# Weight slots and modulated halves moved onto the address grid of the feed-forward tiles

## The chip, the cores and the metric

One NeuronCore of one Trainium2 chip runs the whole program. The metric is device microseconds of one execution, the median of several; the executions of the kernel before lie between 2122.51 and 2123.18 us. The profile is one further execution with the hardware profiler on.

## What is computed

Four decoder layers over 256 tokens of width 1024, in float32. Each layer has three sub-layers: a SwiGLU feed-forward, a token mixer (latent attention, differential attention, Mamba-2, latent attention in layers 0 to 3), and a second feed-forward. Every sub-layer modulates its input by columns that come from a condition vector, and ends in a LayerNorm:

```
def _swiglu(h, w_in, w_out):
    gate, up = jnp.split(h @ w_in, 2, axis=-1)
    return (jax.nn.silu(gate) * up) @ w_out

def _sublayer(x, fn, mod_j, g, b, weight):
    shift, scale, gate = mod_j[:, 0, None, :], mod_j[:, 1, None, :], mod_j[:, 2, None, :]
    y = fn(x * (1 + scale) + shift)
    return _layernorm(DEEPNORM_ALPHA * x + weight * gate * y, g, b)
```

The feed-forward is 1024 to 2 x 2816 and 2816 to 1024, eight times in all. These products, and the mixers' projections, are nearly all of the work.

## The kernel before

**Layout of the data.** Activations lie transposed: features on the 128 partitions, the 256 tokens along the free axis, eight blocks k of 128 features. A matrix product in near-float32 precision is made of three fp32r matmuls (`mm3`, line 475): each operand is split into a high half and a low half, and high x high, high x low and low x high are summed in PSUM. In the rows of the profile the moving operand stands first behind the arrow and the weights second: `mm<-hwh,wr` moves a modulated high half over a weight block.

**The tiles that matter.** `wraw` receives raw weights from HBM. `wr` has 16 slots of 4,096 bytes a partition, each with the high or the low half of four k of one 256-column piece of weights; a matmul takes a block of 128 columns, 512 bytes, so every block starts a multiple of 512 bytes into its slot. `hwh` and `hwl` hold the high and low half of a sub-layer's modulated input, eight rows k one behind the other. `g` has 25 slots of 2,048 bytes, and each half of a feed-forward's hidden tile (two k of 1,024 bytes) fills one; mixers keep their tiles there too.

**Joint first products.** The statistics of a LayerNorm are known late. So the first product of a sub-layer runs on the unnormalized sum, with 258 columns: 256 tokens and two boundary columns that carry the scale and shift terms (`pre_mms`, line 860). `Tail.chunk` writes these wide rows, the boundary columns among them from `abcol` (two strided 128x8 writes for each half). Later, `normalize` (line 847) overwrites the same tiles with the finished modulated input of 256 columns, and all other first products of the sub-layer read that. Before the change both kinds of row start every HP = 288 elements, 1,152 bytes. The very first sub-layer has no joint product; `first_group` (line 698) writes 256-column rows and issues, for each k, 36 matmuls (two halves of the weights, three pieces, two column blocks, three products).

**Order.** All operations are recorded, and a planner with a table of costs lays them out on the engines; the program is then issued in that order. Semaphore waits are set by the framework from what the instructions read and write. First products of a later feed-forward run k by k: in each k six matmuls for one weight piece (two column blocks of three), 12 where two pieces run together. Output products sum over the 22 hidden blocks of 128, three matmuls for each.

**Addresses.** The pools are laid one behind the other in the order in which the code makes them, and the first, `g`, starts at a byte that is 128 modulo 1,024. The slots of `g`, `wraw`, `gacc`, `res`, `t256`, `sd` and `re` are multiples of 1,024 bytes, so all of these start at that remainder. Then come `dtr` (512 bytes), `w0` (128), two `mrows` of 512 and six `modc` of 96: 2,240 bytes, which is 2 x 1,024 + 192. So `wr`, `hwh` and `hwl` start 192 bytes further, at 320 modulo 1,024, and row k of a modulated half starts 128k bytes further again (1,152 = 1,024 + 128).

Of the kernel before, what the change touches and what calls it, by code (L numbers as in the profile page):

```python
# [11 lines left out]
F32R = mybir.dt.float32r  # L12
# [8 lines left out]
S = 256  # L21
L = 4
KD = D // 128
# [396 lines left out]
def trunk(ctx: ExitStack, tc: tile.TileContext, consts, x, c, positions, w_mod, b_mod, ln_g, ln_b,  # L420
# [10 lines left out]
    PW, HP = S + 2, 288  # L431
    slots = {}

    def pool(name, n, elems, dt=F32):
        slots[name] = Slots(sb, name, n, elems, dt=dt, fresh=name == "g")

    slots["mm"] = slots["aux"] = Slots(pp, "mm", 8, 512, True)
    for name, n, elems in (("g", 25, 512), ("wraw", 8, 1024), ("gacc", 1, 1024), ("res", 1, 2048),
                           ("t256", 14, 256), ("sd", 1, 512), ("re", 1, 512), ("dtr", 1, 128), ("w0", 1, 32),
                           ("mrows", 2, 128), ("modc", 6, 24)):  # L440
        pool(name, n, elems)
    for name, n, elems in (("wr", 16, 1024), ("hwh", 1, KD * HP), ("hwl", 1, KD * HP)):
        pool(name, n, elems, F32R)

    def buf(tag, shape, dt=F32):
        return slots[tag].tile(shape, dt)
# [10 lines left out]
    def mmbank(name="pmm"):  # L457
        return buf("mm", [128, 2, 256])

    def aux(name="paux"):  # L460
        return buf("aux", [128, 512])

    def g2(dt=F32, name="g2"):
        return buf("g", [128, 2, 256], dt)
# [4 lines left out]
    def t256(dt=F32, name="t256"):  # L469
        return buf("t256", [128, 256], dt)  # L470

    def f(ap):
        return ap.bitcast(F32)
# [20 lines left out]
    def copy(out, in_):  # L494
        prog.alt((A, "activation", (), dict(out=out, in_=in_, func=AF.Copy)), (V, "tensor_copy", (), dict(out=out, in_=in_)))

    def split(src, hi, lo):
        A.activation(out=hi, in_=src, func=AF.Copy)
        (V.tensor_tensor if src.root.slots.psum else tt)(out=lo, in0=src, in1=f(hi), op=ALU.subtract)

    P_ = {}
    items = []
# [136 lines left out]
    modc = {}  # L639
# [58 lines left out]
    def first_group(res):  # L698

        modc[0] = buf("modc", [128, 24])  # L700
        gm_state["mac"] = 16
        hh, hl = buf("hwh", [128, KD, HP], F32R)[:, :, :S], buf("hwl", [128, KD, HP], F32R)[:, :, :S]
        banks = [mmbank("pf") for _ in range(2 * G0)]
        xr = None
        wv = ffn_w_in[0, 0].rearrange("(k p) (a c) -> k p a c", p=128, a=2)
        for k in range(KD):
            if k % 2 == 0:
                xr = g2(name="xin")
                prog.slack = 0.0 if k else SOON
                Q.dma_start(out=xr, in_=x[0, :, k * 128:k * 128 + 256].rearrange("(t p) c -> p t c", p=128))  # L710
                prog.slack = 0.0
            t = []
            for h in range(2):
                t.append(buf("wraw", [128, 4, 2, 128]))
                for a in range(2):
                    c0 = a * 1024 + k * 128
                    Q.dma_start(out=t[h][:, :, a], in_=w_mod[0, h * 512:h * 512 + 512, c0:c0 + 128].rearrange("(j p) c -> p j c", p=128))
            pg = aux("pgm0")
            prog.bundle(1100.0, [dict(out=pg[32 * (j % 4):32 * (j % 4) + 32, :256], lhsT=condc[:, j:j + 1].to_broadcast([128, 32]),
                                      rhs=t[j // 4][:, j % 4].rearrange("p a c -> p (a c)"), start=(j < 4), stop=(j >= 4)) for j in range(8)])  # L720
            row = t256(name="row0")
            copy(row, pg[:, :256])
            pc = aux("pc0")
            for a in range(2):
                TL.matmul(out=pc[:, a:a + 1], lhsT=row[:, a * 128:a * 128 + 128], rhs=inv32, start=True, stop=True)
            sc = sm_cols[:, k]
            V.scalar_tensor_tensor(out=sc[:, 0:1], in0=pc[:, 1:2], scalar=1.0, in1=bmodc[:, 8 + k:9 + k], op0=ALU.add, op1=ALU.add)
            V.tensor_tensor(out=sc[:, 1:2], in0=pc[:, 0:1], in1=bmodc[:, k:k + 1], op=ALU.add)
            px = aux("pxT")
            for tk in range(2):  # L730
                TL.transpose(px[:, tk * 128:tk * 128 + 128], xr[:, tk, (k % 2) * 128:(k % 2) * 128 + 128], ident)
            A.activation(out=res[:, k], in_=px[:, :S], func=AF.Copy, scale=ALPHA)
            h = t256(name="h")
            V.tensor_scalar(out=h, in0=px[:, :S], scalar1=sc[:, 0:1], scalar2=sc[:, 1:2], op0=ALU.mult, op1=ALU.add)
            split(h, hh[:, k], hl[:, k])
            for a in range(2):
                raw = buf("wraw", [128, G0 * 256])
                Q.dma_start(out=raw, in_=wv[k, :, a, :G0 * 256])
                wh, wl = buf("wr", [128, G0 * 256], F32R), buf("wr", [128, G0 * 256], F32R)
                split(raw, wh, wl)  # L740
                for b in range(G0):
                    for c in range(2):
                        c0 = b * 256 + c * 128
                        mm3(banks[2 * b + a][:, c], wh[:, c0:c0 + 128], wl[:, c0:c0 + 128], hh[:, k], hl[:, k],
                            k == 0 and c == 0, k == KD - 1 and c == 1)
        return hh, hl, banks

    class Tail:
# [4 lines left out]
        def chunk(self, m, ps):  # L753
# [23 lines left out]
            if self.s + 1 == NS:  # L777
                if m == 0:
                    self.banks = [[buf("mm", [128, 512]) for _ in range(2)] for _ in range(2)]
                    self.grow, self.brow = buf("wraw", [128, D]), buf("gacc", [128, D])  # L780
                    Q.dma_start(out=self.grow, in_=ln_g[L - 1, 2:3, :].to_broadcast([128, D]))
                    Q.dma_start(out=self.brow, in_=ln_b[L - 1, 2:3, :].to_broadcast([128, D]))
                dg = t256(name="dg")
                A.activation(out=dg, in_=d[:, m], func=AF.Copy, scale=P_["lngc"][:, self.s * 8 + m:self.s * 8 + m + 1])
                for t in range(2):
                    TL.transpose(self.banks[t][m // 4][:, (m % 4) * 128:(m % 4) * 128 + 128], dg[:, t * 128:t * 128 + 128], ident)
            else:
                first = DEFER.get(self.s, 0)
                if m < first:
                    return  # L790
                if m == first:
                    self.ab = boundary_cols(self.s + 1)
                    self.w = [buf("hw" + n, [128, KD, HP], F32R)[:, :, :PW] for n in "hl"]
                    for q in range(2):
                        A.activation(out=self.w[0][:, :, S + q], in_=self.ab[:, q], func=AF.Copy)
                        V.tensor_tensor(out=self.w[1][:, :, S + q], in0=self.ab[:, q], in1=f(self.w[0][:, :, S + q]), op=ALU.subtract)
                for j in range(0 if m == first else m, m + 1):
                    a = self.ab[:, 0, j:j + 1]
                    A.activation(out=self.w[0][:, j, :S], in_=d[:, j], func=AF.Copy, scale=a)
                    V.scalar_tensor_tensor(out=self.w[1][:, j, :S], in0=d[:, j], scalar=a, in1=f(self.w[0][:, j, :S]),  # L800
                                           op0=ALU.mult, op1=ALU.subtract)
# [37 lines left out]
    class Enter:  # L839
        def __init__(self, s, tail, res):  # L840
            self.s, self.res, self.tail = s, res, tail
            self.ab = tail.ab
            self.wh, self.wl = tail.w
            tail.stats()
            self.R, self.E = tail.re[:, 0], tail.re[:, 1]

        def normalize(self, need_h=True):
            u, ab = self.res, self.ab
            if need_h:
                self.hh, self.hl = self.wh[:, :, :S], self.wl[:, :, :S]  # L850
            for m in range(KD):
                tt(out=u[:, m], in0=u[:, m], in1=self.R, op=ALU.mult)
                tt(out=u[:, m], in0=u[:, m], in1=self.E, op=ALU.add)
                if need_h:
                    h = t256(name="h")
                    act_affine(h, u[:, m], ab[:, 0, m:m + 1], ab[:, 1, m:m + 1])
                    split(h, self.hh[:, m, :S], self.hl[:, m, :S])
            for m in range(KD):
                act_affine(u[:, m], u[:, m], ab[:, 2, m:m + 1], ab[:, 3, m:m + 1])
        def pre_mms(self, *ws):  # L860
# [730 lines left out]
    tail, res = None, buf("res", [128, KD, S])  # L1591
    for s in range(NS):
        en = Enter(s, tail, res) if s else None
        kind = "ffn" if s % 3 != 1 else MIXERS[s // 3]
        tail = Tail(s, res, 0.5 if kind == "ffn" else 1.0)
# [35 lines left out]
```

## Time and profile before

| | us |
|---|---|
| median of three runs | 2123.11 |
| the profiled execution, its own time | 2126.3 |
| its span, first to last instruction | 2124.5 |
| TensorE matmuls busy | 2097.0 (99%) |
| VectorE busy | 1723.4 (81%) |
| ScalarE busy | 1186.8 (56%) |
| moved from and to HBM | 504.73 MB, 238 GB/s in the mean |

Matmuls overlap in the engine, and the end of each is modelled. So the length that the profile lists for one is longer than the time until the next one starts, and the busy share says little of how fast TensorE goes. What tells it is the distance from one start to the next, which is read from the timeline: a row there gives the start of a run of equal instructions, its length and their number. All instructions stand on line 396, the one line that issues them; groups are told apart by tile names.

### The profile page before, as it was taken

What the parts mean: (1) busy time and instruction counts of PE and PEld (TensorE: products, weight loads), DVE (VectorE), ACT (ScalarE), POOL (GpSimd) and SP (SyncE); (2) the same over time, 40 slices, a digit from 0 to 9 for tenths busy, and PEclk for the clock granted to TensorE, in tenths of its full rate; (3) what the DMA queues carried; (4) which work ended last, traced back from release to release, by engine and by line L of the source; (5) the groups of instructions that cost most, each with busy time, mean ns of one, the idle gap of its engine ahead of it and who ended that gap; (6) DMA issues with size and microseconds to landing.
All of it is one profiled execution on the core that took longest, in us unless ns stands there. A gap on an engine that the chain in (4) does not pass through costs nothing.

```text
span 2124.5 us, 43163 instructions
## 1 busy us (share of the span) xinstructions
PE 2097.0 (99%) x17398; PEld 2027.6 (95%) x17398; DVE 1723.4 (81%) x2739; ACT 1186.8 (56%) x1853; POOL 96.0 (5%) x112
## 2 busy tenths in 40 slices
PE   8999999999999999999999999999999999999998
PEld 6999999999999999999999988899999999999998
DVE  3788999878887868978987898879887888879744
ACT  3553687446544776544644575547545644577543
POOL 0000110000000101000000011000000000100000
PEclk9999999999999999999999999999999999999999
DMA  9899667887899534899588744345897789545851
GB/s 293 275 330 327 216 209 247 291 305 217 280 315 319 174 103 148 302 314 314 191 304 308 249 141 143 115 156 196 303 315 226 258 309 316 178 131 187 258 184 55
DMA packets 410636, 504.73 MB, mean 238 GB/s; under 512 B 22073, under 2 KB 371652, under 8 KB 410436
## 3 DMA queue, kind: packets, MB, share of 16 engines
q1 hardware_dynamic: 410436, 501.98, 71.4%
q8 instruction: 136, 2.23, 0.4%
q14 instruction: 64, 0.52, 0.1%
HBM read 500.73 MB, written 1.05 MB: 236 GB/s over the span
## 4 chain that ended last, share of the span: by engine, by line
PE 93%; DVE 4%; issue 1%; ACT 1%; DMA 0%; POOL 0%; SPq 0%; DVEq 0%; POOLq 0%; ACTq 0%
PE mm L396 93%; DVE res L396 1%; DVE t L396 1%; DVE wr L396 1%; DVE sd L396 0%; DVE g L396 0%; DVE hwl L396 0%; DMA wraw<-in_w_mod_dram 0%; ACT t L396 0%; ACT g L396 0%; ACT wr L396 0%; SPq L396 0%; POOL rs L396 0%; ACT L396 0%; DVE gacc L396 0%
## 5 line engine op out<-in xcount | busy, mean ns | idle before, releaser
L396 PE MATMUL mm<-hwh,wr 128*128 128x256 f32 (+1 forms) x6736 | 1234.7, 284 | 3.7 <-ACT hwh L396 1.9
L396 PEld LDWEIGHTS mm<-hwh,wr 128*128 128x128 f32 x6736 | 1045.4, 189 | 24.4 <-issue 18.2
L396 ACT ACTIVATE wr<-wraw 128x1024 fp32r<-128x1024 f32 (+3 forms) x705 | 700.7, 1003 | 621.1 <-DMA wraw<-in_ffn_w_in_dram 190.4
L396 PE MATMUL mm<-hwl,wr 128*128 128x256 f32 (+1 forms) x3368 | 960.1, 285 | 3.3 <-DVE hwl L396 3.1
L396 DVE TENSOR_TENSOR wr<-wraw,wr 128x1024 fp32r<-128x1024 f32 (+3 forms) x693 | 796.8, 1167 | 166.7 <-ACT wr L396 160.3
L396 PE MATMUL mm<-g,wr 128*128 128x256 f32 x5496 | 671.6, 281 | 1.6 <-DVE g L396 0.9
L396 PEld LDWEIGHTS mm<-g,wr 128*128 128x128 f32 x5496 | 655.0, 188 | 11.8 <-issue 6.9
L396 PEld LDWEIGHTS mm<-hwl,wr 128*128 128x128 f32 x3368 | 637.6, 189 | 9.2 <-DVE hwl L396 5.1
L396 DVE SCALAR_TENSOR_TENSOR gacc<-wraw,condc,gacc 128x1024 f32<-128x1024 f32 x238 | 305.9, 1285 | 4.7 <-DMA wraw<-in_w_mod_dram 2.2
L396 ACT ACTIVATE g<-mm 128x512 f32<-128x512 f32 (+4 forms) x209 | 105.4, 517 | 51.0 <-PE mm L396 49.2
L396 ACT ACTIVATE g<-g 128x512 fp32r<-128x512 f32 (+1 forms) x104 | 63.7, 625 | 37.8 <-DVE g L396 37.3
L396 PE MATMUL mm<-g,g 128*128 128x128 f32 (+2 forms) x464 | 81.8, 312 | 0.0
L396 DVE TENSOR_TENSOR g<-g,g 128x512 fp32r<-128x512 f32 (+2 forms) x114 | 75.3, 686 | 3.4 <-ACT g L396 2.3
L396 DVE TENSOR_TENSOR res<-res,re 128x256 f32<-128x256 f32 x168 | 66.9, 420 | 8.6 <-ACT re L396 8.2
L396 POOL TENSOR_TENSOR res<-res,t 128x256 f32<-128x256 f32 x31 | 28.4, 943 | 914.9 <-ACT t L396 914.9
L396 DVE TENSOR_TENSOR g<-g,mm 128x512 f32<-128x512 f32 x81 | 54.4, 682 | 14.9 <-PE mm L396 14.5
L396 ACT ACTIVATE t<-mm 128x256 f32<-128x256 f32 (+1 forms) x72 | 27.1, 377 | 68.8 <-PE mm L396 68.5
L396 PEld LDWEIGHTS mm<-g,g 128*128 128x128 f32 (+1 forms) x464 | 57.9, 175 | 7.2 <-ACT g L396 0.4
L396 ACT ACTIVATE t<-res 128x256 f32<-128x256 f32 x84 | 34.6, 416 | 51.9 <-DVE res L396 42.2
L396 DVE SCALAR_TENSOR_TENSOR res<-mm,gw,res 128x256 f32<-128x256 f32 x84 | 39.5, 478 | 16.9 <-PE mm L396 16.4
L396 ACT ACTIVATE t<-res,abcol 128x256 f32<-128x256 f32 x72 | 43.1, 599 | 8.1 <-DVE res L396 6.8
L396 ACT ACTIVATE res<-res,abcol 128x256 f32<-128x256 f32 x88 | 47.5, 589 | 0.0
(200 smaller groups left out, 1165.1 us busy)
## 6 DMA issues: line engine op xcount, KB each, us to landing
wraw<-in_ffn_w_in_dram SPq DMA_DIRECT2D x340, 512.0 KB
wraw<-in_w_mod_dram SPq DMA_DIRECT2D x272, 512.0 KB
wraw<-in_ffn_w_out_dram SPq DMA_DIRECT2D x128, 512.0 KB
wraw<-in_ffn_w_out_dram SPq DMA_DIRECT2D x64, 384.0 KB
wraw<-in_ssm_w_in_dram SPq DMA_DIRECT2D x32, 512.0 KB
wraw<-in_diff_w_in_dram SPq DMA_DIRECT2D x24, 512.0 KB
wraw<-in_w_mod_dram SPq DMA_DIRECT2D x32, 256.0 KB
wraw<-in_mla_w_out_dram SPq DMA_DIRECT2D x16, 512.0 KB
```

Of the source, the lines that this page charges most:

```text
L396: getattr(eng.real, method)(*[real(a) for a in args], **{k: real(v) for k, v in one.items()})
```

## The change

The four pools whose sizes are no multiple of 1,024 bytes (`dtr`, `w0`, `mrows`, `modc`) are made after `wr`, `hwh` and `hwl` instead of before. These three start 192 bytes lower, at 128 modulo 1,024 as `g` does. A new function `modulated()` makes each of the two modulated tiles once and gives two views of it: wide rows of 258 columns every 1,152 bytes, for the joint products, and narrow rows of 256 columns every 1,024 bytes, for everything else. `normalize`, `first_group` and all first products after the joint ones use the narrow rows; the joint products use the wide rows as before. Wide and narrow rows share the same bytes.

```diff
@@ -436,11 +436,12 @@
     for name, n, elems in (("g", 25, 512), ("wraw", 8, 1024), ("gacc", 1, 1024), ("res", 1, 2048),
-                           ("t256", 14, 256), ("sd", 1, 512), ("re", 1, 512), ("dtr", 1, 128), ("w0", 1, 32),
-                           ("mrows", 2, 128), ("modc", 6, 24)):
+                           ("t256", 14, 256), ("sd", 1, 512), ("re", 1, 512)):
         pool(name, n, elems)
     for name, n, elems in (("wr", 16, 1024), ("hwh", 1, KD * HP), ("hwl", 1, KD * HP)):
         pool(name, n, elems, F32R)
+    for name, n, elems in (("dtr", 1, 128), ("w0", 1, 32), ("mrows", 2, 128), ("modc", 6, 24)):
+        pool(name, n, elems)
@@ -497,6 +498,11 @@
+    def modulated():
+
+        flat = [buf("hw" + n, [128, KD * HP], F32R) for n in "hl"]
+        return [[a[:, :KD * p].rearrange("p (k n) -> p k n", k=KD)[:, :, :n] for a in flat] for p, n in ((HP, PW), (S, S))]
@@ -699,7 +705,7 @@
-        hh, hl = buf("hwh", [128, KD, HP], F32R)[:, :, :S], buf("hwl", [128, KD, HP], F32R)[:, :, :S]
+        hh, hl = modulated()[1]
@@ -790,7 +796,7 @@
-                    self.w = [buf("hw" + n, [128, KD, HP], F32R)[:, :, :PW] for n in "hl"]
+                    self.w, self.h = modulated()
@@ -841,20 +847,19 @@
             self.wh, self.wl = tail.w
+            self.hh, self.hl = tail.h
...
-            if need_h:
-                self.hh, self.hl = self.wh[:, :, :S], self.wl[:, :, :S]
...
-                    split(h, self.hh[:, m, :S], self.hl[:, m, :S])
+                    split(h, self.hh[:, m], self.hl[:, m])
```

Every engine issues the same operations in the same order as before. What differs beside the addresses is a few waits. ScalarE, at the end of differential attention's V product: `hwh<-abcol` is the write of a boundary column of the next sub-layer, `g<-mm` the eviction of a V tile or of scores. Before:

```order
L396 ACTIVATE g_9021<-mm_68,sublnc_171 128x256 [waits PE_49]
L396 ACTIVATE g_9029<-mm_67,sublnc_171 128x256 [waits PE_49]
L396 ACTIVATE hwh_146<-abcol_183 128x8
L396 ACTIVATE g_9004<-mm_63 128x256 [waits PE_49]
L396 ACTIVATE g_9051<-mm_66,drs_238 128x128 [waits PE_49]
```

The same place after the change:

```order
L396 ACTIVATE g_9021<-mm_68,sublnc_171 128x256 [waits PE_49]
L396 ACTIVATE g_9029<-mm_67,sublnc_171 128x256 [waits PE_49]
L396 ACTIVATE hwh_136<-abcol_183 128x8 [waits PE_49]
L396 ACTIVATE g_9004<-mm_63 128x256 [waits PE_49]
L396 ACTIVATE g_9051<-mm_66,drs_238 128x128 [waits PE_49]
```

The boundary column now lies in the bytes of narrow rows, so its write waits for TensorE, the reader of those rows. ScalarE gets this wait at one more place and VectorE at two, each at such a 128x8 write; two writes of weight slots behind ScalarE's other one lose theirs.

## Rows read from the trace of the kernel before

**Rows 1.** The page, parts 1 and 4: busy time by engine; the chain by engine.

```profile
PE 2097.0 (99%) x17398; PEld 2027.6 (95%) x17398; DVE 1723.4 (81%) x2739; ACT 1186.8 (56%) x1853; POOL 96.0 (5%) x112
...
PE 93%; DVE 4%; issue 1%; ACT 1%; DMA 0%; POOL 0%; SPq 0%; DVEq 0%; POOLq 0%; ACTq 0%
```

**Rows 2.** Two stretches of feed-forwards by engine: first products, then output products.

```profile
core 0: us, PE busy (x) PEld busy (x) DVE busy (x) ACT busy (x) POOL busy (x), PEclk, DMA share, GB/s
...
340.00:450.00 110.00, 110.00 (x934) 108.20 (x934) 93.27 (x105) 58.01 (x75) 0.00 (x0) 1.00 0.87 303
...
452.00:512.00 60.00, 60.00 (x511) 59.25 (x511) 48.66 (x68) 30.04 (x41) 2.74 (x3) 1.00 0.87 288
```

**Rows 3.** TensorE's groups by form; behind the bar busy us, mean ns, idle us before.

```profile
L396 PE MATMUL mm<-hwh,wr 128*128 128x256 f32 x5984 | 1095.5, 284 | 3.7 <-ACT hwh L396 1.9 <-ACT g L396 0.9 <-DVE wr L396 0.5
L396 PE MATMUL mm<-hwl,wr 128*128 128x256 f32 x2992 | 851.3, 285 | 1.8 <-DVE hwl L396 1.8
L396 PE MATMUL mm<-g,wr 128*128 128x256 f32 x5496 | 671.6, 281 | 1.6 <-DVE g L396 0.9 <-ACT g L396 0.3 <-DVE modc L396 0.2
L396 PE MATMUL mm<-hwh,wr 128*128 128x258 f32 x752 | 140.5, 285 | 0.0
L396 PE MATMUL mm<-hwl,wr 128*128 128x258 f32 x376 | 108.8, 289 | 1.5 <-DVE hwl L396 1.4
...
L396 PE MATMUL mm<-cst,g 128*128 128x128 f32 x140 | 28.9, 279 | 2.2 <-DMA g<-in_x_dram 1.0 <-ACT g L396 0.6 <-DVE g L396 0.5
L396 PE MATMUL mm<-wr,hwh 128*128 128x256 f32 x128 | 26.8, 300 | 0.0
L396 PE MATMUL mm<-gacc,ones 128*32 128x256 f32 x272 | 21.7, 391 | 0.0
L396 PE MATMUL mm<-wr,hwl 128*128 128x256 f32 x64 | 19.2, 300 | 0.0
L396 PE MATMUL mm<-wr,g 128*128 128x512 f32 x48 | 18.0, 459 | 0.0
...
L396 PE MATMUL mm<-maskb,identb 128*128 128x128 bf16 x64 | 14.4, 225 | 0.0
```

**Rows 4.** Timeline of TensorE, first group, k = 6 and 7: start us, length, what.

```profile
59.31 0.40 PE L396 MATMUL mm<-hwh,wr 128*128 128x256 f32 x2
59.55 0.28 PE L396 MATMUL mm<-hwl,wr 128*128 128x256 f32 x1
...
62.06 0.28 PE L396 MATMUL mm<-hwl,wr 128*128 128x256 f32 x1
...
62.42 0.28 PE L396 MATMUL mm<-hwl,wr 128*128 128x256 f32 x1
...
66.34 0.28 PE L396 MATMUL mm<-hwl,wr 128*128 128x256 f32 x1
66.46 0.28 PE L396 MATMUL mm<-hwh,wr 128*128 128x256 f32 x1
```

**Rows 5.** Timeline of TensorE: first and last low-half matmul, last feed-forward's first products.

```profile
1935.67 0.28 PE L396 MATMUL mm<-hwl,wr 128*128 128x256 f32 x1
...
2048.99 0.28 PE L396 MATMUL mm<-hwl,wr 128*128 128x256 f32 x1
```

**Rows 6.** Timeline of TensorE: three runs of output products from g tiles.

```profile
1572.56 23.36 PE L396 MATMUL mm<-g,wr 128*128 128x256 f32 x197
...
1824.73 5.33 PE L396 MATMUL mm<-g,wr 128*128 128x256 f32 x43
...
1211.52 5.15 PE L396 MATMUL mm<-g,wr 128*128 128x256 f32 x43
```

**Rows 7.** Timeline of TensorE: 512-column matmuls of latent attention's V.

```profile
1869.10 1.57 PE L396 MATMUL mm<-wr,g 128*128 128x512 f32 x6
```

**Rows 8.** Timeline at the end of differential attention's V product: TensorE, then ScalarE.

```profile
802.25 0.28 PE L396 MATMUL mm<-wr,hwl 128*128 128x256 f32 x1
...
801.75 0.21 ACT L396 ACTIVATE hwh<-abcol 128x8 fp32r<-128x8 f32 x1
802.56 0.38 ACT L396 ACTIVATE g<-mm 128x256 f32<-128x256 f32 x1 [0.61 <-PE mm L396]
```

## The prediction

> **What bounds the kernel now.** I read the page's first and fourth part first: TensorE is busy for 2097.0 of 2124.5 us and holds 93% of the chain that ended last [rows 1]. Then two stretches by engine: in the first products of a feed-forward and in an output product TensorE is busy all the time at the full granted clock (1.00, the 2.4 GHz level), VectorE for 81 to 85% of it (48.66 of 60, 93.27 of 110 us), the DMA engines for 0.87 [rows 2]. Nothing feeds TensorE late there, so the time is the number of matmuls times the spacing of their starts. The question is that spacing alone. The listed length of a matmul (281 to 285 ns) is no spacing: they overlap.
>
> The groups by form give the numbers: 5,984 + 2,992 matmuls of 256 columns whose moving operand is a modulated half (hwh, hwl), 5,496 from the feed-forward and mixer tiles (g), 1,128 joint ones of 258 columns, and few others in fp32r [rows 3].
>
> Now the spacing, from starts. It differs, for one form of instruction at one clock. In the first group of the program 36 matmuls stand on each k, in order of k, and the last starts at 66.46 us. In k = 6 the seven triples from 59.55 to 62.06 take 0.36 us each, 120.0 ns a matmul, one like the other; in k = 7, the last 36, the eleven triples from 62.42 to 66.34 take 3.92 us, 118.8 ns [rows 4]. Over the 960 first-product matmuls of the last feed-forward, where k moves on every six, 957 starts take 2048.99 - 1935.67 = 113.32 us, 118.4 ns [rows 5]. Output products from g: (23.36 - 0.28)/196 = 117.8 ns. But of two runs of 43 g matmuls at the same place in two feed-forwards one takes 5.33 and the other 5.15 us: 0.18/42 = 4.3 ns less each, so some 113.5 where the other has 117.8 [rows 6].
>
> So spacing depends on addresses and on how the run started. What separates the three kinds is how far the moving row starts from the weight block that loads beside it, taken modulo 256 bytes (weight blocks are multiples of 512 bytes into a slot). A modulated row k lies 1,152k bytes into its tile, and its tile has the same remainder as the weight slots: distance 0 for even k, 128 for odd k. A g tile lies 192 bytes off the weight slots: distance 64. Rows: 0 locks at 120.0, 128 wanders around 118.8, 64 locks at 117.8 and now and then at 113.5. That two reads of one memory hold each other up when they march over the same banks would do this; no row shows banks, so this is a reading.
>
> **The change part by part.** No instruction is added, dropped or put elsewhere. Three things change.
>
> 1. The weight slots, hwh and hwl move down by 192 bytes and now have the remainder of the g tiles. For g the distance becomes 0. If distance decides, its spacing goes from 117.8 to 120.0: 5,496 x 2.2 ns = +12.1 us. Bounds: 0 (nothing about g itself moved) and +12.1; runs at 113.5 are left out, being few. I take +12.1, since the row with distance 0 is the nearest to what is built.
>
> 2. Narrow rows of 1,024 bytes. Every modulated row outside the joint products has then the weight slots' remainder, odd k too: distance 0 throughout. From the mean of 118.4 to the lock of 120.0: 8,976 x 1.6 = +14.4 us. The wandering was worth something: after a step of k some starts come early, and with one distance for all k there is no step. Bounds: 118.4 to 117.8 if a row's own address decides (-5.4), and +14.4. I take the upper.
>
> 3. Joint rows keep 1,152 bytes and their distance to the weights, 128k: 0. Bound: 2 ns on 1,128 either way, 2.3 us.
>
> The small rest: 192 matmuls with weights and modulated rows in exchanged roles (diff's V), 192 x 1.6 = 0.3 at most; 48 of 512 columns at about (1.57 - 0.4)/5 = 234 ns, which twice 120 would raise by 48 x 6 = 0.3 [rows 3, 7]; together +0.6. Against it stands the settling after an interruption: in the k = 6 block the starts from 59.31 to 59.55 come before the lock, about 2 ns early each [rows 4]. Other matmuls cut into these runs some 200 times (272/8 blocks of gacc, 140 transposes of g in pairs, 64 masks, and pieces of the mixers [rows 3]), at two to five early starts: -0.8 to -2.0 us, an estimate from those rows; I take -2.0.
>
> Waits: narrow and wide rows now overlap, so the boundary columns of the next sub-layer (hwh, hwl from abcol, 128x8) wait for the last reader of the narrow rows. One place is near: ScalarE writes them at 801.75, TensorE's last read there starts at 802.25 and ends at 802.53. Queued behind it on ScalarE is the eviction that starts at 802.56 after waiting for TensorE anyway [rows 8]. So ScalarE waits some 0.8 us, 0.61 of which it idles today, and the eviction and the attention product that reads it slip by 0 to 0.3 us; with that cover gone it would be the whole 0.8. I take 0.2. The others come after the last read, and cost nothing. A normalized row k overlaps joint rows k - 1 and k only, which are read by then as before. Transfers keep their order and have more time; VectorE, ScalarE and SP are not the bound [rows 2].
>
> Sum: 12.1 + 14.4 + 0.6 + 0.2 - 2.0 = **+25.3 us**. TensorE idles 3.7 + 1.8 + 1.6 us before all the matmuls of the three large groups [rows 3], so next to nothing is absorbed; I drop 0.7. On the profiled execution, whose span is 2124.5: 2126.3 + 24.6 = 2150.9; that execution lies 3.2 us above the median of the runs, 2123.1, so the forecast is **2147.7 us**. Its own range: 2136 (g stays, only the halves lock) to 2153 (no settling, joint rows 2 ns worse).
>
> **A rule that says otherwise.** The rows have one form of matmul at 120.0, 118.8, 117.8 and 113.5 ns [rows 4, 6]. The Trainium skill, "TensorE: Matmul & The Clock Gate", section "Step-by-step: what each phase is for", says that TensorE reads moving data and weights through two independent ports, so that a weight load takes nothing from a running matmul; by that no distance matters, the sum is 0. The rows differ from this: something that goes with addresses and with the start does hold the matmuls up.
>
> **Rivals.**
> *The row's own place decides, not the distance* (faster). What g has that the halves lack is its remainder, 128 modulo 1,024 bytes, at a multiple of 128. Then g keeps 117.8 and the halves join it: -0.6 x 8,976 = -5.4 us, joint rows up to -2.3 more. 2115.4 to 2117.7, say 2116.5. For it: g is even over all its slots, whatever block it meets. Against: even and odd k are both 64 bytes off such a multiple and still differ [rows 4].
> *The other lock.* g has two steady spacings, and a new layout could settle on the lower: -4.9 x 8,976 - 4.3 x 5,496 = -67.6 us, 2055.5; the DMA engines, at 0.87 of those stretches, would be at 0.91 (0.87 x 118.4/113.5), so 2055 to 2064. Against: distance 0 has not shown it in a long run, and g rarely.
> *No effect.* If the differences come from which accumulators follow each other (both halves of a bank in turn in the first products, one after all k in parts of the output products) and not from addresses, nothing changes, for that order is the same: 2123.1. Against: k = 6 and k = 7 have the same order and differ [rows 4]. The page cited above gives this result too.
>
> **How the numbers follow.** Distance decides, as in the sum: 0.68; the row's own place: 0.18; the other lock: 0.08; no effect: 0.06. A measurement of this kernel tells about 0.2% (4.2 us) from no change. The first is slower, the second and third faster, the fourth the same: faster 0.26, same 0.06, slower 0.68. The range takes the forecast's own, no effect and the second case, and leaves out the other lock and the tails: 2113 to 2153.
>
> **What would show it.** The last feed-forward's first products: 957 spacings in 114.8 us (distance), 112.7 (own place), 108.6 (other lock), 113.3 (no effect). The g run of 197: 23.8 us against 23.4. In both the matmul groups keep their listed lengths of 281 to 285 ns within a few, their counts exactly. If g reads 117.8 while the halves read 120.0, distance is wrong for g and the time is near 2136. ScalarE's 128x8 write at 801.75 should stand just behind TensorE's last read. The forecast is wrong altogether if a lock below 117 holds for whole stages.

## The result, and the profile after

| | before | after |
|---|---|---|
| median, us | 2123.14 (2122.51 to 2123.32) | 2147.02 (2146.24 to 2148.95) |
| ratio, 95% interval | | 1.0112 (1.0099 to 1.0124) |
| profiled execution, its own time / span, us | 2126.3 / 2124.5 | 2147.0 / 2145.2 |

The changed kernel is slower by 23.9 us. The forecast was 2147.7, from the theory that the distance between moving rows and weight blocks sets the spacing of matmuls.

The page of the kernel after, parts 1 and 4:

```profile
PE 2121.0 (99%) x17398; PEld 2053.0 (96%) x17398; DVE 1723.6 (80%) x2739; ACT 1185.9 (55%) x1853; POOL 97.1 (5%) x112
...
PE 92%; DVE 4%; issue 2%; ACT 1%; DMA 1%; POOL 0%; SPq 0%; DVEq 0%; POOLq 0%; ACTq 0%
```

Against [rows 1], every engine issues the same number of instructions, VectorE and ScalarE are busy for the same time within 1 us, and TensorE is busy for 24.0 us more. So the other engines do no more work; TensorE itself takes longer for the same matmuls.

Two stretches of feed-forwards by engine, after (busy us and, in brackets, instructions of PE, PEld, DVE, ACT, POOL; granted clock, DMA share, GB/s):

```profile
340.00:450.00 110.00, 110.00 (x922) 108.21 (x921) 92.00 (x104) 58.04 (x75) 0.00 (x0) 1.00 0.87 300
452.00:512.00 60.00, 60.00 (x502) 59.25 (x502) 48.69 (x67) 29.81 (x41) 2.75 (x3) 1.00 0.87 292
```

TensorE is never idle and its granted clock is 1.00, both as in [rows 2]. But 922 matmuls fit into the 110 us where 934 did, and 502 into the 60 us where 511 did: 1.3 and 1.8% fewer at the same clock.

TensorE's groups by form, after (behind the bar busy us, mean ns, idle us before):

```profile
L396 PE MATMUL mm<-hwh,wr 128*128 128x256 f32 x5984 | 1108.8, 286 | 3.1 <-ACT hwh L396 1.9 <-ACT g L396 0.9 <-DVE mkg L396 0.3
L396 PE MATMUL mm<-hwl,wr 128*128 128x256 f32 x2992 | 855.9, 286 | 1.8 <-DVE hwl L396 1.8
L396 PE MATMUL mm<-g,wr 128*128 128x256 f32 x5496 | 683.6, 285 | 1.6 <-DVE g L396 0.9 <-ACT g L396 0.3 <-DVE modc L396 0.2
L396 PE MATMUL mm<-hwh,wr 128*128 128x258 f32 x752 | 140.6, 285 | 0.0
```

Counts are those of [rows 3], and the idle times differ from them by 0.6 us at most, so nothing feeds TensorE later. The listed length of one matmul rises by 1 to 4 ns in the three large groups and says little, as before. The joint products (last line; 140.5 us before, 140.6 now) stand still.

Where the time is shows in the starts. Timeline of TensorE and, at 808 us, of ScalarE, after (start us, length, what):

```profile
56.85 0.28 PE L396 MATMUL mm<-hwl,wr 128*128 128x256 f32 x1
57.21 0.28 PE L396 MATMUL mm<-hwl,wr 128*128 128x256 f32 x1
57.56 0.28 PE L396 MATMUL mm<-hwl,wr 128*128 128x256 f32 x1
...
59.72 0.28 PE L396 MATMUL mm<-hwl,wr 128*128 128x256 f32 x1
...
63.68 0.28 PE L396 MATMUL mm<-hwl,wr 128*128 128x256 f32 x1
63.80 0.28 PE L396 MATMUL mm<-hwh,wr 128*128 128x256 f32 x1
...
807.82 0.28 PE L396 MATMUL mm<-wr,hwl 128*128 128x256 f32 x1
808.02 0.22 ACT L396 ACTIVATE hwh<-abcol 128x8 fp32r<-128x8 f32 x1 [0.59 <-PE mm L396]
808.13 0.38 ACT L396 ACTIVATE g<-mm 128x256 f32<-128x256 f32 x1
...
1222.14 5.41 PE L396 MATMUL mm<-g,wr 128*128 128x256 f32 x43
...
1586.36 23.80 PE L396 MATMUL mm<-g,wr 128*128 128x256 f32 x197
...
1842.19 5.41 PE L396 MATMUL mm<-g,wr 128*128 128x256 f32 x43
...
1886.90 1.55 PE L396 MATMUL mm<-wr,g 128*128 128x512 f32 x6
...
1953.70 0.28 PE L396 MATMUL mm<-hwl,wr 128*128 128x256 f32 x1
...
2068.53 0.28 PE L396 MATMUL mm<-hwl,wr 128*128 128x256 f32 x1
```

- k = 7 of the first group, 59.72 to 63.68: eleven triples in 3.96 us, 120.0 ns a matmul, where [rows 4] had 118.8 for the same 33. The odd k now runs as the even k did.
- The last feed-forward's first products: 957 spacings in 2068.53 - 1953.70 = 114.83 us, 120.0 ns; [rows 5] had 113.32 us.
- The run of 197 output products: (23.80 - 0.28)/196 = 120.0 ns; [rows 6] had 117.8. The two runs of 43 that differed before are alike now, 5.41 us each, (5.41 - 0.28)/42 = 122 with the interruption's edge.

Summed over all starts of the trace, from each start to the next one of TensorE (less than 135 ns apart counts as a back-to-back pair; the rest are gaps, where something else stands between). The numbers of pairs are those after the change:

| | before, ns | after, ns | difference, us |
|---|---|---|---|
| halves, 8,692 back-to-back pairs | 118.43 | 119.91 | +12.2 |
| g, 5,360 pairs | 117.66 | 119.92 | +12.1 |
| joint, 1,083 pairs | 120.69 | 120.73 | +0.3 |
| gaps in the three | | | -1.4 |
| all else | | | -2.5 |
| span | | | +20.7 |

Five of the halves' pairs count among the gaps after the change, so the first difference is 0.6 us below (119.91 - 118.43) x 8,697. The last line but one is, in the main, the start of the program: the first group ends at 63.80 us, at 66.46 in [rows 4], 2.66 us earlier although its matmuls are slower, so the waits before and inside it took that much less in this execution. That differs from one execution to the next: in the fourteen traces of this case the first matmul with a modulated half starts between 13.0 and 14.7 us, and the first group ends between 61.9 and 66.9 us. From the end of the first group on, the difference is (2145.2 - 63.80) - (2124.5 - 66.46) = 23.4 us, close to the 23.9 of the medians.

### The profile page after: what moved, and what is told of

Same layout as the page of the kernel before. It is cut to its first block, busy times and chain, and to the rows that moved or that the text cites. A ratio compares the mean times of both kernels' runs of the same rounds, so it can differ in the third digit from the quotient of the medians.

```text
span 2145.2 us, 43163 instructions
## 1 busy us (share of the span) xinstructions
PE 2121.0 (99%) x17398; PEld 2053.0 (96%) x17398; DVE 1723.6 (80%) x2739; ACT 1185.9 (55%) x1853; POOL 97.1 (5%) x112
## 4 chain that ended last, share of the span: by engine, by line
PE 92%; DVE 4%; issue 2%; ACT 1%; DMA 1%; POOL 0%; SPq 0%; DVEq 0%; POOLq 0%; ACTq 0%
PE mm L396 92%; DVE res L396 1%; DVE t L396 1%; DVE wr L396 1%; DVE sd L396 0%; ACT t L396 0%; DVE g L396 0%; DMA g<-in_x_dram 0%; DMA wraw<-in_w_mod_dram 0%; ACT g L396 0%; SPq L396 0%; ACT wr L396 0%; DVE gacc L396 0%; DVE hwl L396 0%; POOL rs L396 0%
## 5 line engine op out<-in xcount | busy, mean ns | idle before, releaser
L396 PE MATMUL mm<-hwh,wr 128*128 128x256 f32 (+1 forms) x6736 | 1248.0, 286 | 3.1 <-ACT hwh L396 1.9
L396 PEld LDWEIGHTS mm<-hwh,wr 128*128 128x128 f32 x6736 | 1059.0, 192 | 23.3 <-issue 18.2
L396 PE MATMUL mm<-g,wr 128*128 128x256 f32 x5496 | 683.6, 285 | 1.6 <-DVE g L396 0.9
L396 PEld LDWEIGHTS mm<-g,wr 128*128 128x128 f32 x5496 | 667.0, 192 | 11.7 <-issue 6.9
L396 PEld LDWEIGHTS mm<-hwl,wr 128*128 128x128 f32 x3368 | 647.1, 192 | 7.8 <-DVE hwl L396 3.7
L396 DVE TENSOR_TENSOR res<-res,re 128x256 f32<-128x256 f32 x168 | 66.9, 420 | 8.5 <-ACT re L396 8.0
L396 DVE TENSOR_SCALAR gacc<-wraw,condc 128x1024 f32<-128x1024 f32 x28 | 21.1, 754 | 36.9 <-PE mm L396 35.9
```

Of the source, the lines that this page charges most:

```text
L396: getattr(eng.real, method)(*[real(a) for a in args], **{k: real(v) for k, v in one.items()})
```

## The experiments

The theory: the distance of the moving row from the weight block, modulo 256 bytes, sets the spacing. The rivals: the row's own place sets it, or the order of accumulators does. In the traces each kernel below, apart from the last one, has the instructions of the changed kernel in the same order on every engine, only with other addresses. "Cadence" is the mean of the back-to-back pairs, worked out from all starts as above. The kernel before took 2122.85 to 2123.27 us in the median of each of these comparisons, and single executions of it 2122.29 to 2125.62 us.

### Each half of the change alone

Narrow rows alone, with the small pools back ahead of the weight slots (against the changed kernel):

```diff
-    for name, n, elems in (("wr", 16, 1024), ("hwh", 1, KD * HP), ("hwl", 1, KD * HP)):
-        pool(name, n, elems, F32R)
-    for name, n, elems in (("dtr", 1, 128), ("w0", 1, 32), ("mrows", 2, 128), ("modc", 6, 24)):
-        pool(name, n, elems)
+    for name, n, elems, dt in (("dtr", 1, 128, F32), ("w0", 1, 32, F32), ("mrows", 2, 128, F32), ("modc", 6, 24, F32), ("wr", 16, 1024, F32R), ("hwh", 1, KD * HP, F32R), ("hwl", 1, KD * HP, F32R)):
+        pool(name, n, elems, dt)
```

> Half of the change alone: narrow rows of 1,024 bytes, but the pools stay where they were (weight slots and halves 192 bytes off the g tiles). Distance between moving row and weight block, modulo 256: halves 0 for every k, g tiles 64. If distance decides: halves lock at 120.0 ns, g stays at 117.8, time 2123.1 + 14.4 - 1 = about 2136 us. If a row's or a slot's own place decides (all halves and weights are, as before, 64 bytes off a multiple of 128): near 2123.

Measured: 2135.27 us, 1.0055 (1.0040 to 1.0070) of the kernel before. Timeline of TensorE, narrow rows alone: first and last low-half matmul of the last feed-forward's first products, and the run of 197 from g.

```profile
1942.27 0.28 PE L396 MATMUL mm<-hwl,wr 128*128 128x256 f32 x1
...
2057.10 0.28 PE L396 MATMUL mm<-hwl,wr 128*128 128x256 f32 x1
...
1577.53 23.37 PE L396 MATMUL mm<-g,wr 128*128 128x256 f32 x197
```

Halves: 114.83 us, 120.0 ns; g: (23.37 - 0.28)/196 = 117.8, as before. The halves lock and g stays, which the distance says and the row's own place does not.

The move of the pools alone, on the kernel before, with rows of 1,152 bytes everywhere:

```diff
-                           ("t256", 14, 256), ("sd", 1, 512), ("re", 1, 512), ("dtr", 1, 128), ("w0", 1, 32),
-                           ("mrows", 2, 128), ("modc", 6, 24)):
+                           ("t256", 14, 256), ("sd", 1, 512), ("re", 1, 512)):
...
+    for name, n, elems in (("dtr", 1, 128), ("w0", 1, 32), ("mrows", 2, 128), ("modc", 6, 24)):
+        pool(name, n, elems)
```

> The other half alone: pools moved, so weight slots and halves have the remainder of g, but modulated rows keep 1,152 bytes. Distances: halves 0 for even k and 128 for odd k as before, g tiles 0 instead of 64. If distance decides: halves stay at a mean of 118.4 ns, g locks at 120.0, time 2123.1 + 12.1 - 1 = about 2134 us. If a moving row's own place decides: g has not moved and keeps 117.8, the halves stand at multiples of 128 and go to 120, about 2136 us but with the gain and loss in the other groups.

Measured: 2134.75 us, 1.0053 (1.0038 to 1.0068). The same three rows, pools moved alone:

```profile
1943.90 0.28 PE L396 MATMUL mm<-hwl,wr 128*128 128x256 f32 x1
...
2057.22 0.28 PE L396 MATMUL mm<-hwl,wr 128*128 128x256 f32 x1
...
1578.10 23.78 PE L396 MATMUL mm<-g,wr 128*128 128x256 f32 x197
```

The mirror image: the halves keep 113.32 us, 118.4 ns, and g goes to (23.78 - 0.28)/196 = 119.9, though no g tile has moved by a byte. Only the weights beside it have. The two parts cost 12.4 and 11.9 us over the 2122.86 of the kernel before in this comparison, 24.3 together, against 23.9 for both at once: they add up.

### Everything 64 bytes further

A pad ahead of all these pools, which keep their order (against the changed kernel):

```diff
+    pool("pad", 1, 16)
     for name, n, elems in (("g", 25, 512), ("wraw", 8, 1024), ("gacc", 1, 1024), ("res", 1, 2048),
...
```

> The changed kernel with 64 bytes put ahead of all pools: every tile moves by 64 bytes, no distance changes. If distance decides: 120.0 ns in both groups, 2147 us, as the changed kernel. If places decide: all of them are now 64 bytes off a multiple of 128, as weights and even halves were before, so the spacings change, back towards 118 ns and 2123 us.

Measured: 2146.51 us, 1.0108 (1.0091 to 1.0125). The same three rows:

```profile
1955.10 0.28 PE L396 MATMUL mm<-hwl,wr 128*128 128x256 f32 x1
...
2069.93 0.28 PE L396 MATMUL mm<-hwl,wr 128*128 128x256 f32 x1
...
1587.77 23.80 PE L396 MATMUL mm<-g,wr 128*128 128x256 f32 x197
```

114.83 us and 23.80 us, as in the changed kernel. Halves, g tiles and weight slots all stand at other places, all distances are the same, and so is the spacing. Together with the two halves of the change this rules the row's own place out.

### Other distances

Here `hwh` and `hwl` stand first behind the unchanged pools, so that halves and g have one remainder, and `wr` is put at a chosen distance by what lies between. For 64 bytes (against the changed kernel):

```diff
-    for name, n, elems in (("wr", 16, 1024), ("hwh", 1, KD * HP), ("hwl", 1, KD * HP)):
-        pool(name, n, elems, F32R)
-    for name, n, elems in (("dtr", 1, 128), ("w0", 1, 32), ("mrows", 2, 128), ("modc", 6, 24)):
-        pool(name, n, elems)
+    for name, n, elems, dt in (("hwh", 1, KD * HP, F32R), ("hwl", 1, KD * HP, F32R), ("dtr", 1, 128, F32), ("w0", 1, 32, F32), ("mrows", 2, 128, F32), ("modc", 6, 24, F32), ("wr", 16, 1024, F32R)):
+        pool(name, n, elems, dt)
```

The others differ in what stands between `hwl` and `wr`: `w0` (128 bytes) for 128; a pad of 64 bytes for 192; a pad of 32 ahead of the four small pools for 32; `w0` and a pad of 32 for 96; pads of 64 and 32 for 160; a pad of 32 for 224.

64 bytes:

> The changed kernel with the weight slots alone put 192 bytes off: halves (narrow rows) and g tiles both at distance 64. If distance decides: both groups at the 117.8 ns that g had (or, in runs that start so, at 113.5), so 2147 - 2.2 ns x 14,472 = 2115 to 2118 us, faster than both kernels; the joint products, now at 64 and 192 in place of 0 and 128, may add or take 2 us. If weights at multiples of 128 were the harm and not distance: 117.8 as well, so this one is the candidate and not the test.

128 bytes:

> All moving rows outside the joint products, halves and g tiles, at distance 128 from the weight blocks. Before, odd k stood there: no lock, a mean of 118.8 ns over a block of equal k. If distance decides: 118.8 in both groups, 2147 - 1.2 x 14,472 = 2130 us, between the changed kernel and the one before. If only multiples of 256 are harmful and anything else does as well as 64: about 2111.

192 bytes:

> All of them at distance 192. Not seen before for 256 columns; the 512-column matmuls stood at it (about 234 ns, the same per column as 117). If the two streams only repel near distance 0 and the order does not matter, 192 mirrors 64: 117.4 ns and 2111 us. If who leads matters, a lock of its own, anywhere from 113.3 (2055 us) to 120.0 (2147 us).

32 bytes:

> All of them at distance 32, half of the step of 64 bytes in which distances differed so far. If what collides are pieces of 64 bytes or more, 32 behaves as 0 or as 64: 120.0 ns and 2147 us, or 117.4 and 2111. If smaller pieces collide, a value of its own.

96 bytes:

> All of them at distance 96. By pieces of 64 bytes it behaves as 64 or as 128: 117.4 ns and 2111 us, or 118.8 and 2130; by smaller pieces a value of its own.

160 bytes:

> All moving rows outside the joint products at distance 160. So far: 0 locks at 120.0 ns, 32 gives 117.1, 64 two locks (117.8 and 113.3, mean 117.4), 96 wanders around 120.0, 128 around 118.7, 192 has the same two locks as 64, with 113.3 in over half of the matmuls (mean 115.3). If 32 steps behave like the 64 they belong to (0 with 96?) no order is to be seen; if the price is a smooth function of distance: between 118.7 and 115.3, so about 117 ns and 2107 us.

224 bytes:

> All of them at distance 224, that is 32 behind the next 0. A smooth function would put it between 192 (115.3) and 0 (120.0): about 117.6 ns and 2115 us. If 224 is to 192 as 32 is to 64 (32 wanders where 64 locks): the mean of 192 without the locks, 115 to 117 ns and 2085 to 2108 us.

Measured, with the changed kernel as distance 0 (two executions each at 96 and 192, three at 32, four or eight at the others):

| distance | time, us | ratio to before, interval | cadence halves / g, ns | how the starts come |
|---|---|---|---|---|
| 0 | 2147.02 | 1.0112 (1.0099 to 1.0124) | 119.91 / 119.92 | 120 each |
| 32 | 2111.13 | 0.9942 (0.9919 to 0.9965) | 117.23 / 117.00 | 113 to 120, changing |
| 64 | 2111.30 | 0.9944 (0.9929 to 0.9959) | 117.35 / 117.37 | 117.8, in 10% below 115 |
| 96 | 2146.56 | 1.0112 (1.0083 to 1.0142) | 119.94 / 119.94 | 115 to 125, changing |
| 128 | 2130.85 | 1.0034 (1.0015 to 1.0054) | 118.70 / 118.67 | 115 to 122, changing |
| 160 | 2120.95 | 0.9990 (0.9978 to 1.0001) | 118.11 / 117.95 | 115 to 122, changing |
| 192 | 2086.07 | 0.9828 (0.9799 to 0.9856) | 115.25 / 115.38 | 113.3 in over half, else 117.8 |
| 224 | 2125.16 | 1.0006 (0.9995 to 1.0017) | 118.35 / 118.34 | 115 to 123, changing |

The run of 197 at each, timeline of TensorE. At 32 bytes:

```profile
1560.59 23.14 PE L396 MATMUL mm<-g,wr 128*128 128x256 f32 x197
```

At 64 bytes, with the first and the last low-half matmul of the last feed-forward:

```profile
1560.47 23.36 PE L396 MATMUL mm<-g,wr 128*128 128x256 f32 x197
...
1921.71 0.28 PE L396 MATMUL mm<-hwl,wr 128*128 128x256 f32 x1
...
2034.42 0.28 PE L396 MATMUL mm<-hwl,wr 128*128 128x256 f32 x1
```

At 96 bytes:

```profile
1586.31 23.80 PE L396 MATMUL mm<-g,wr 128*128 128x256 f32 x197
```

At 128 bytes, with the same two matmuls of the last feed-forward:

```profile
1577.54 23.53 PE L396 MATMUL mm<-g,wr 128*128 128x256 f32 x197
...
1942.09 0.28 PE L396 MATMUL mm<-hwl,wr 128*128 128x256 f32 x1
...
2055.66 0.28 PE L396 MATMUL mm<-hwl,wr 128*128 128x256 f32 x1
```

At 160 bytes:

```profile
1568.31 23.28 PE L396 MATMUL mm<-g,wr 128*128 128x256 f32 x197
```

At 224 bytes:

```profile
1570.71 23.47 PE L396 MATMUL mm<-g,wr 128*128 128x256 f32 x197
```

What follows. First, in each of these eight kernels halves and g, which have one distance there, have the same cadence within 0.25 ns: 2034.42 - 1921.71 = 112.71 us and (23.36 - 0.28)/196 give 117.8 both at 64 bytes, 113.57 us and 23.53 us give 118.7 and 118.6 at 128. So the accumulators' order, which differs between first and output products, has next to no say.

Second, the time moves from 2147 down to 2086 us by addresses alone. Third, that nearer means slower, in some even way, is wrong: 96 is as slow as 0, 192 is not the mirror of 64, and no rule for the eight values was found.

Of the expectations, 128 bytes was met (2130 us) and 32 came out at one of its two values (2111); 64 lies 4 us below its 2115, since a tenth of its pairs ran below 115 ns; 96 (2111 or 2130), 160 (2107) and 224 (2115, or 2085 to 2108) were missed.

The uneven rows of the kernel before ran at 118.43, below both kinds they are made of (120.0 at 0, 118.7 at 128): changing k is worth about 1 ns against the mean of the two, 119.3.

That the distance counts modulo 256 bytes, and not 512, the table can't say: in all kernels of it but the first the weight block starts 32 to 224 bytes behind the row, modulo 512, so each distance stands there once. Two other readings say it. In [rows 4] the row k = 6 stands 256 bytes off the weights modulo 512 and has 120.0 ns, as distance 0 has. And in differential attention's V product weights and modulated rows have exchanged roles. Its 192 matmuls so stand at the opposite distance: at 32 in the kernel for 224, which modulo 512 is 256 bytes away from the table's 32, and likewise for the others. Their back-to-back pairs, 152 or 153 in each trace, come to 117.05 ns at 32, 119.61 at 96, 118.91 at 128, 118.26 at 160 and 118.40 at 224, each within 0.4 ns of the halves and g at that distance in the table. At 64 and 192, where two spacings share the time, they come to 118.00 and 117.73, above the table's 117.4 and 115.3. One thing stays open: in the kernel before, the last feed-forward's spacings repeat every four k and not every two (118.3 ns in the mean at k = 1 and 5, 118.9 at k = 3 and 7), so what came before carries over, or 512 has some part.

### The fastest distance again

The same program as at 192 bytes, in another comparison.

> Distance 192 once more, timed more often. If the share of matmuls that run at 113.3 ns is set by chance at each interruption, runs scatter by a few us around 2086 and the share in the profile differs from the 57% of the first; the result stays 1.5 to 1.9% faster than before. If the first was a lucky phase, it comes out up to 2112, the time with all at 117.8.

Measured: 2089.25 us (2085.90 to 2093.64), 0.9839 (0.9825 to 0.9853). It stays well below every other distance, but 42% of the halves' pairs are at 113, where it was 58%. Timeline and two stretches of the first profiled execution at 192 bytes (the run of 197 from g; first and last low-half matmul of the last feed-forward's first products; then 1645 to 1740 us, first products up to some 1730 us and output products behind, and 1930 to 2000 us, all first products of the last feed-forward; columns as above):

```profile
1541.01 22.49 PE L396 MATMUL mm<-g,wr 128*128 128x256 f32 x197
...
1899.14 0.28 PE L396 MATMUL mm<-hwl,wr 128*128 128x256 f32 x1
...
2007.60 0.28 PE L396 MATMUL mm<-hwl,wr 128*128 128x256 f32 x1
```

```profile
1645.00:1740.00 95.00, 95.00 (x822) 93.37 (x822) 79.29 (x81) 44.55 (x55) 0.00 (x0) 1.00 0.90 312
1930.00:2000.00 70.00, 70.00 (x620) 70.00 (x619) 50.91 (x53) 36.60 (x44) 1.43 (x1) 1.00 0.78 256
```

The same of the second execution:

```profile
1543.81 22.49 PE L396 MATMUL mm<-g,wr 128*128 128x256 f32 x197
...
1902.04 0.28 PE L396 MATMUL mm<-hwl,wr 128*128 128x256 f32 x1
...
2014.75 0.28 PE L396 MATMUL mm<-hwl,wr 128*128 128x256 f32 x1
```

```profile
1645.00:1740.00 95.00, 95.00 (x821) 93.37 (x820) 79.60 (x84) 45.86 (x57) 0.00 (x0) 1.00 0.90 312
1930.00:2000.00 70.00, 70.00 (x596) 70.00 (x596) 49.57 (x51) 36.20 (x45) 1.33 (x1) 1.00 0.74 242
```

The run of 197 stands at (22.49 - 0.28)/196 = 113.3 ns in both. In the last feed-forward the 957 spacings take 2007.60 - 1899.14 = 108.46 us in one execution and 2014.75 - 1902.04 = 112.71 us in the other, 113.3 against 117.8 ns (620 and 596 matmuls in the 70 us), with the same instructions, addresses and clock and no idle time. So this distance has two steady spacings. Which one holds is settled where matmuls start anew behind an interruption: of the 96 and 95 uninterrupted runs of at least 20 pairs in the two traces, none changes from one to the other. Of the 24 stretches of first, joint and output products with at least 100 pairs, 14 have the same share of 113 in both executions within one point, 10 don't.

### Joint rows at the fastest distance too

Wide rows every 1,280 bytes put the joint rows at 192 bytes as well; two of the `t256` slots pay for it, and a few operations move or change engine (VectorE 2,737 instructions, ScalarE 1,855).

```diff
-    PW, HP = S + 2, 288
+    PW, HP = S + 2, 320
...
-                           ("t256", 14, 256), ("sd", 1, 512), ("re", 1, 512)):
+                           ("t256", 12, 256), ("sd", 1, 512), ("re", 1, 512)):
```

> Distance 192 for the joint rows as well: wide rows every 1,280 bytes (a multiple of 256), the room taken from two of 14 t256 buffers, which moves some instructions of the normalization. If distance decides for 258 columns too: 119.8 goes to 114 to 118.7 ns on 1,128 matmuls, 1 to 6 us faster than distance 192 alone, so about 2082 us. If the two lost buffers cost a wait at each of eleven sub-layer borders, that is given back: 2086 or more.

Measured: 2078.66 us (2077.34 to 2081.74), 0.9793 (0.9780 to 0.9806) of the kernel before, the fastest version here: 44.6 us below it and 68.4 below the changed kernel. But not for the reason it was made: the joint products went from 119.80 to 120.66 ns, not down. Timeline and the two stretches:

```profile
1537.37 22.49 PE L396 MATMUL mm<-g,wr 128*128 128x256 f32 x197
```

```profile
1645.00:1740.00 95.00, 95.00 (x845) 92.85 (x844) 80.82 (x81) 44.47 (x55) 0.00 (x0) 1.00 0.92 311
1930.00:2000.00 70.00, 70.00 (x620) 70.00 (x619) 46.87 (x50) 35.34 (x42) 0.00 (x0) 1.00 0.75 246
```

The first stretch holds 845 matmuls where the two executions before had 822 and 821: the 960 first products that it mostly holds came to a mean of 117.1 ns there and come to 113.4 here. 87% of the halves' pairs are at 113. The gain is in the stretches behind the joint products. Whether the joint rows' other spacing or the few moved operations set this off was not separated.

## Why the prediction was right

**The theory.** Distance decides, for matmuls of 256 columns: shown by the two halves of the change, which each slowed only the kind whose distance they changed, g without moving it, and by the shift of everything, which changed nothing. It does not decide alone, as the two spacings at 192 bytes show, and for the 258-column joint products it is not shown. What inside holds the matmuls up is open: that two reads collide was a reading, and no run here shows it.

**g, +12.1.** Measured +12.1 in the trace, +11.9 alone. The 117.8 left out the few runs at 113.5; the measured mean with them was 117.66, and the settling took off about what they added.

**Halves, +14.4.** Measured +12.2 in back-to-back pairs, 12.4 alone. Counted too high because 284 of the 8,976 stand before a gap and do not lengthen (0.5 us), the mean before was 118.43 (0.3 us), five pairs moved to the gaps (0.6 us), and some starts come early (0.8 us): the -2.0 for settling was meant for that. Settling: 119.91 and 119.92 instead of 120.0, 0.8 + 0.4 = 1.2 us, in the first triples after an interruption, as 56.85, 57.21 and 57.56 above show (0.36 and 0.35 us).

**Joint, 0.** Measured +0.3 in pairs and -1.3 in gaps, inside the bound of 2.3.

**Small rest, +0.6.** Wrong in part. The 192 matmuls of diff's V went from 118.7 to 119.5 ns, +0.15 us. The 512-column ones became faster: 1.55 us for six, about 230 ns, against 1.57 in [rows 7]. "Twice 120" does not hold for them; 0.2 us the other way.

**ScalarE's wait, +0.2.** Measured 0. The write at 808.02 now waits, 0.59 us, for TensorE's last read, which starts at 807.82; the eviction behind it starts at 808.13, 0.31 us after that read. In [rows 8] it is 802.56 - 802.25 = 0.31 too. The write took the place of the eviction's own wait.

**Absorbed, -0.7, and the 3.2 us to the median.** The gaps of the three groups gave back 1.4 us. That the profiled execution before lay 3.2 us above its median fits its start: it ends its first group 2.66 us later than the one after, which lies at its median, and the one at 128 bytes, with the latest end of all (66.90 us), lies 2.6 us above its own. The executions that were not profiled left no trace, so this is not shown.

**The total.** Halves and g with their settling were put at 24.5 us and came to 24.3. What was put at 0.1 (small rest, ScalarE's wait, absorbed) came to -1.1 with the joint products and all gaps, and the 3.2 us between the profiled execution before and its median to 2.5 (all else, in the table above). These two misses are of opposite sign, so it is partly luck that the forecast came within 0.7 us.

**The rule of no effect.** Counts, order and clock are the same in the kernels from 2086 to 2147 us; only addresses differ. The Trainium skill, "TensorE: Matmul & The Clock Gate", section "Step-by-step: what each phase is for", says that a weight load takes no read bandwidth from a running matmul; by that all of these would take the same time. Whatever the cause inside, for fp32r matmuls of 256 columns with a weight load to each, the measurement decides against equal times.

**The rival "other lock"** did not come true in this kernel: at distance 0 no long run settled below 120. But its lower spacing is real: at 192 bytes it holds whole stretches, and the time (2079 to 2089 us) went well below anything the row's own place would have given. The DMA engines, which the rival put at 0.91, did not stop it: their share is 0.92 in the last kernel's stretch from 1645 us, with TensorE busy throughout and the first products there at 113.4 ns.

## What to carry to other kernels

When TensorE is busy all the time and its granted clock is 1.00, take the spacing of starts, not the listed length, and compare it between forms and tiles: a difference at equal columns can be time to be had. Then try the byte distance of moving operand and weight block, which costs a pad between two pools; measure it, since no simple rule held, and do not expect a tidy grid to be the good one: here it was the worst of eight, together with 96. Where two spacings occur in one program, repeat the measurement, since which stretch gets which can change from one execution to the next.

## What the runs showed that was not expected

- At one clock and one form (256 columns, fp32r) the mean spacing lies between 115.3 and 119.9 ns by the distance modulo 256 bytes, from 2147 to 2086 us for the whole kernel; 96 gives the mean of distance 0 without its evenness.
- At 192 bytes two steady spacings, 113.3 and 117.8 ns, exist for the same program: 108.46 or 112.71 us for the same 957 spacings.
- Joint matmuls of 258 columns gained nothing from 192 bytes: 120.66 ns, against 119.80 with rows at 64 and 192 in turn.
- The distance counts modulo 256 bytes from either side: with weights and rows exchanged, differential attention's V runs at 117.05 ns at 32 bytes and 119.61 at 96, close to the halves there (117.23, 119.94).
- Open: what inside makes them slower, what picks the spacing at the start of a run, and steps finer than 32 bytes, which were not tried.
